# Moving the rotation DMAs to GpSimd and widening the step distances of a hand-ordered two-layer decoder kernel

## The chip, the cores and the metric

The kernel runs on one core of one Trainium2 chip. The metric is the device time of one execution in microseconds (us), as the median of several executions. A profiled execution has a span, from the first instruction to the last one of the core, and a time of its own that is a little longer than the span.

## What is computed

Two layers of a decoder step for one prompt of 512 tokens and eight sample sequences of 4 tokens, which share all weights; the 544 token columns are handled together, in two halves of 272. Everything is float32. A layer is, in short:

```python
h = rmsnorm(x, norm1_g) * (1 + mod[:, 1]) + mod[:, 0]
z = h @ w_in
yA = pool_mixer(z[..., COL_POOL:COL_RET], ...)        # sliding means
q, kr = rotary(zr[:, :, 0], pos), rotary(zr[:, :, 1], pos) * (RET_DK ** -0.5)
yB = retention(q, kr, zr[:, :, 2], st_ret)            # normed, times silu gate
conv_y, n_sc = causal_dwconv(zc[..., 2 * MIX_W:] * zc[..., :MIX_W], st_sc, sc_w)
yC = zc[..., MIX_W:2 * MIX_W] * conv_y
yD = rwkv7_mixer(z[..., COL_RWKV:COL_GATE], ...)      # delta-rule scan over tokens
mixed = jnp.sum(gates * einsum(branches, w_br), axis=2) @ w_out
x = x + mod[:, 2] * mixed
h2 = rmsnorm(x, norm2_g) * (1 + mod[:, 4]) + mod[:, 3]
up = causal_dwconv(h2 @ w_up, st_ffn, ffn_w)
x = x + mod[:, 5] * ((silu(up[..., :D_FF]) * up[..., D_FF:]) @ w_down)
```

`mod` comes from a product of the conditioning with `w_ada`, which the kernel works out beside the rest. The new states of all mixers are outputs too.

## The kernel before

**Large products.** Activations lie with channels on the partitions. A weight arrives in units of 128x1024 (eight tiles of 128x128); its raw copy (three buffers) is split on chip into a high part (a cast on ScalarE, L130) and a low part (a subtraction, L134, on VectorE, for weights 1 and 2 of the start on GpSimd), with four buffer pairs for split weights. Each tile product is three matmuls, high by high, high by low and low by high (L164, L165, L166, `mm3`), on one half of 272 columns. There are 13,248 of these large matmuls. A unit of input projection is 24 large matmuls for each half. Their sums go into three PSUM buffers (`pd`); the small products of the mixers use five others (`pm`).

**The order is written by hand.** Every engine but the DMA-issuing SyncE runs its instructions in the order in which the program emits them. The program counts large matmuls (`nmm`, three at each `mm3`), and after each `mm3` it emits what has come due (`slot`): closures put off by `later(n, ...)` by n large matmuls, and steps of generators, which end in `yield n`. A step thus stands n large matmuls behind the one before, rounded up to the next multiple of three. `yield n, True` marks a step that starts with small matmuls; with a negative n the step is emitted ahead of the others that are due. A distance gives the other engines time to finish what TensorE reads next. `finish` runs what is left of a generator at once.

**The stages of a layer.** First come the eight RWKV input units. Then the generator `rwkv` runs beside the other units: decays and products (`products`, ending in L558, which the small matmuls of L579 read), a substitution of 31 steps on VectorE, and a scan of 16 chunks. A scan chunk goes around TensorE and VectorE: L734 makes `psG`, L696 copies it, L701 multiplies, L705 copies it back, L754 makes the new state, L767 on VectorE adds the decayed old state into `z`, which the next L734 reads; L770 on GpSimd prepares the decayed state `pt` for the chunk after. Beside it come the short convolution, the pooling, their gates (`gates`), and the eight retention units. Of these the first two of each half of the heads, q and k, are rotated: the unit lands in `qn` (L1329), four DMAs (L1338) copy it into `qs` with blocks of 32 partitions swapped, L1339 (VectorE) multiplies `qn` by a cosine table, L1340 (GpSimd) `qs` by a sine table, and L1341 (VectorE) adds both. The tables come by a GpSimd DMA (L1323) for each such unit. After the last chunk GpSimd issues the output of the state (L793) and clears two tiles (L796), which L800 reads; then `retentions` runs. The rest is the output projection, the second norm, and the feed-forward part: up units, whose results go through `conv3` (L1148, L1151, L1152), a silu (L1407), a product (L1411, L1413) and a split (L456, L457), and down products in four parts. A down group is 24, 12, 12 or 18 large matmuls in the four parts, and each ends in a residual on VectorE (L408, L412, L415), which frees its PSUM buffer.

**Norms.** `both_halves` runs eight groups for each half and sums squares (L322, L325); the norm of the first half (`norm_half`: reciprocal L355, multiply L361, scale L338, split L366 and L369) is emitted step by step beside the second half's groups.

**The start.** The first modulation, its eight parts of 1 MB, and the first norm run tile by tile with the first three weight units (`first_units`); weight 3 (the fourth) is loaded when the first three units are done.

Of the kernel before, what the change touches and what calls it, by code (L numbers as in the profile page):

```python
# [24 lines left out]
NU = 138  # L25
D_G, D_S, D_P = 14, 14, 18
KAPPA = -math.exp(-0.5)
# [16 lines left out]
def tile_hybrid_step(ctx: ExitStack, tc: tile.TileContext, io: dict):  # L44
# [305 lines left out]
    def norm_half(xt, half, acc, sA, shA, hh):  # L350

        c0, c1 = HS[half]
        rs = rstd_sqrt(acc)
        yield -8
        V.reciprocal(rs, rs)  # L355
        yield -10
        us = {}
        for i in range(11):
            if i < 8:
                us[i] = ZR(HALF)  # L360
                V.tensor_tensor(out=us[i], in0=xk(xt, i)[:, c0:c1], in1=rs, op=MUL)  # L361
            if 0 <= i - 1 < 8:
                mod_samples(us[i - 1], i - 1, half, sA, shA)
                mod_prompt(us[i - 1], i - 1, half, sA, shA)
            if 0 <= i - 2 < 8:
                S.copy(hilo_of(i - 2, half, hh)[0], us[i - 2])  # L366
            if 0 <= i - 3:
                hi, lo = hilo_of(i - 3, half, hh)
                V.tensor_tensor(out=lo, in0=us[i - 3], in1=hi, op=SUB)  # L369
            yield -11 if half == 0 else -7  # L370

# [87 lines left out]
    def rwkv(l, za, zb, M, yD):  # L459
# [104 lines left out]
        bkn = products(0, e1)  # L564
        yield 44, True
        for T in range(5):
# [35 lines left out]
            if T < 4:  # L602
                yield -14
                bkn = products(T + 1, e1)
                yield 40, True
        rks = []
# [52 lines left out]
        for s in range(31):  # L659
            substitute(s)  # L660
            if s % 2:
                yield -20, False, s > 28
        for h in range(2):
# [142 lines left out]
        for p in range(2):  # L806
# [6 lines left out]
            Zxs.append(Zx)  # L813
        yield 44, True
        psY = PM()
# [46 lines left out]
    def retention(l, p, rt, M, yB):  # L862
# [19 lines left out]
        for ps in pss:  # L882
# [3 lines left out]
            sms.append(sm)  # L886
        yield 24, True
        ps = PM()
# [19 lines left out]
        for T in range(1, 4):  # L908
# [6 lines left out]
                        in1=cst[0:64, C_BM:C_BM + 8].unsqueeze(2).broadcast_to([64, NB, 64]), op=MUL)  # L915
        yield 24, True
        psO = PM()
# [31 lines left out]
        G.dma_start(io["o_ret_s"][l, :, p], S0)  # L949
        yield 24  # L950
        rs = ZR(TOK)
# [74 lines left out]
    for k in range(8):  # L1026
        if k + 4 < 8:
            raw_first(k + 4)
        if k:
            next(afs[k])  # L1030
        if k >= 2:
            first_units(k - 2)
        next(afs[k])
        for half in (1, 0):
            mod_samples(xh0[k][half], k, half, scl[0][:, 0], mods[0][:, 0:8, :])
            mod_prompt(xh0[k][half], k, half, scl[0][:, 0], mods[0][:, 0:8, :])
        if k < 7:
            normed(k + 1)
        for half in range(2):
            hi, lo = hilo_of(k, half, hh)  # L1040
            S.copy(hi, xh0[k][half])
            V.tensor_tensor(out=lo, in0=xh0[k][half], in1=hi, op=SUB)
        if k < 2:
            for _ in range(1 + k):
                load_next(0)
# [7 lines left out]
    for l in range(L):  # L1053
# [91 lines left out]

        def conv3(u, wcol):
            cv = ZR(560)
            S.activation(cv, u[:, 0:560], AF.Copy, scale=wcol(0))  # L1148

            def rest():  # L1150
                V.scalar_tensor_tensor(out=cv, in0=u[:, 1:561], scalar=wcol(1), in1=cv, op0=MUL, op1=ADD)  # L1151
                V.scalar_tensor_tensor(out=cv, in0=u[:, 2:562], scalar=wcol(2), in1=cv, op0=MUL, op1=ADD)  # L1152
            later(5, rest)
            return cv
# [157 lines left out]
        for j, uid in enumerate(RET_UNITS):  # L1312
# [23 lines left out]
            if kind < 2:  # L1336
                for blk in range(4):
                    S.dma_start(qs[32 * blk:32 * blk + 32, :], qn[32 * (blk ^ 1):32 * (blk ^ 1) + 32, :])  # L1338
                V.tensor_tensor(out=qn, in0=qn, in1=tb[0], op=MUL)  # L1339
                later(20, lambda qs=qs, t=tb[1]: G.tensor_tensor(out=qs, in0=qs, in1=t, op=MUL))  # L1340
                later(36, lambda o=rt[:, kind, :], qn=qn, qs=qs: V.tensor_tensor(out=o, in0=qn, in1=qs, op=ADD))  # L1341
            done(l, ui - 1)
# [56 lines left out]
        def finish_up(j):  # L1399
            cvs = []  # L1400
            for s in range(2):
                wc = P_FFW + 3 * (22 * s + j)
                cvs.append(conv3(upads.pop((j, s)), lambda t, wc=wc: par[:, wc + t:wc + t + 1]))
            if j % 2 == 0:
                acts[j // 2] = T4(F32R)
            a = acts[j // 2]
            later(22, lambda: S.activation(cvs[0], cvs[0], AF.Silu))  # L1407

            def product():
                pr = ZR(TOK)  # L1410
                V.tensor_tensor(out=pr[:, 0:SEQ], in0=cvs[0][:, 0:SEQ], in1=cvs[1][:, 0:SEQ], op=MUL)  # L1411
                sv = [cv[:, 512:560].rearrange("p (b t) -> p b t", t=6)[:, :, 2:6] for cv in cvs]
                V.tensor_tensor(out=smp(pr[:, SEQ:TOK]), in0=sv[0], in1=sv[1], op=MUL)  # L1413
                later(8, lambda: split_hilo(pr, a[:, 2 * (j % 2), :], a[:, 2 * (j % 2) + 1, :]))
            later(30, product)

# [284 lines left out]
```

## Time and profile before

| what | value |
|---|---|
| median of 3 runs | 2018.62 us (2017.16 to 2023.3) |
| profiled execution, its own time | 2021.17 us |
| its span | 2019.4 us |
| mean granted TensorE clock | 0.983 |
| VectorE busy | 1098.5 us (54%) |
| ScalarE busy | 807.6 us (40%) |
| GpSimd busy | 236.8 us (12%) |
| HBM read | 213.33 MB, 110 GB/s over the span |

TensorE is PE in the profile, its weight loads PEld, VectorE DVE, ScalarE ACT, GpSimd POOL, SyncE SP; a q behind a name is that engine's queue when it issues DMAs. Idle time of an engine is put down to what ended it, the releaser. PEclk is the share of full clock that TensorE was granted in a stretch.

### The profile page before, as it was taken

The page shows a single profiled execution, that of the slowest core. Times are in us where ns is not written, and L with a number is a line of the kernel's source. Part 1 is how long each engine was busy: PE and PEld are TensorE (multiplying, and loading weights), DVE is VectorE, ACT ScalarE, POOL GpSimd, SP SyncE. Part 2 cuts the span into 40 slices and gives each one's busy share as a digit, 9 for nine tenths or more (in the row PEclk, how much of TensorE's full clock was granted, in tenths as well). Part 3 has the DMA queues.
Part 4 walks back from the last instruction along what each step waited for, and adds up shares of the span by engine and source line. Part 5 has one row for each costly group of instructions (what it writes and reads, how often), then busy time and mean ns, then how long its engine had stood idle before and what let it go on. Part 6 is the DMA issues. An engine that isn't in the chain of part 4 may idle for free. (4 is left out here: it accounts for less than half of the span.)

```text
span 2019.4 us, 39097 instructions
## 1 busy us (share of the span) xinstructions
PE 1927.6 (95%) x16188; PEld 1847.3 (91%) x16188; DVE 1098.5 (54%) x2245; ACT 807.6 (40%) x1578; POOL 236.8 (12%) x655
## 2 busy tenths in 40 slices
PE   6999998999999999999989999999899999999997
PEld 5989997879999998899989899988899999999997
DVE  4455754443466553455664667554435755445565
ACT  4543232253355431434345433333524554243432
POOL 1100033212000000000101001442110000000000
PEclk9999999999999999999999999999999999999998
DMA  7223434422334258522332133232124222222221
GB/s 304 86 74 116 129 117 147 139 81 89 128 112 147 78 206 320 200 84 85 106 118 85 54 95 89 65 119 88 59 94 144 86 74 86 100 85 76 94 93 45
DMA packets 75554, 227.15 MB, mean 112 GB/s; under 512 B 20208, under 2 KB 23072, under 8 KB 73584
## 3 DMA queue, kind: packets, MB, share of 16 engines
q1 hardware_dynamic: 69872, 210.43, 31.0%
q0 software_dynamic: 3536, 11.53, 1.7%
q10 hardware_dynamic: 1968, 2.69, 0.5%
q8 instruction: 127, 2.08, 0.4%
q14 instruction: 51, 0.42, 0.1%
HBM read 213.33 MB, written 9.06 MB: 110 GB/s over the span
## 5 line engine op out<-in xcount | busy, mean ns | idle before, releaser
L164 PE MATMUL pd<-t,whi 128*128 128x272 f32 x4104 | 1212.5, 295 | 20.8 <-DVE t L408 9.3
L166 PE MATMUL pd<-t,wlo 128*128 128x272 f32 x4104 | 1194.6, 291 | 4.6 <-POOL wlo L134 2.4
L165 PE MATMUL pd<-t,whi 128*128 128x272 f32 x4104 | 1188.7, 290 | 4.4 <-DVE t L369 3.9
L164 PEld LDWEIGHTS pd<-t,whi 128*128 128x128 f32 x4104 | 780.4, 190 | 55.1 <-issue 22.6
L165 PEld LDWEIGHTS pd<-t,whi 128*128 128x128 f32 x4104 | 782.2, 191 | 7.0 <-DVE t L369 4.8
L166 PEld LDWEIGHTS pd<-t,wlo 128*128 128x128 f32 x4104 | 780.7, 190 | 5.8 <-POOL wlo L134 3.1
L134 DVE TENSOR_TENSOR wlo<-raw,whi 128x1024 fp32r<-128x1024 f32 x256 | 321.6, 1257 | 125.6 <-ACT whi L130 123.4
L130 ACT CAST whi<-raw 128x1024 fp32r<-128x1024 f32 x258 | 270.7, 1051 | 169.5 <-PE pd L165 142.1
L1151 DVE SCALAR_TENSOR_TENSOR zr<-zr,par,zr 128x560 f32<-128x560 f32 x92 | 73.5, 799 | 165.2 <-ACT zr L1148 165.2
L1247 ACT ACTIVATE zr<-pd 128x272 f32<-128x272 f32 x128 | 50.7, 397 | 225.1 <-PE pd L166 213.9
L1395 ACT COPY zr<-pd 128x272 f32<-128x272 f32 (+2 forms) x264 | 72.5, 310 | 155.6 <-PE pd L166 155.6
L408 DVE SCALAR_TENSOR_TENSOR t<-pd,mod,t 128x272 f32<-128x272 f32 (+1 forms) x160 | 76.4, 481 | 92.3 <-PE pd L166 92.2
L1397 POOL COPY off<-zr 128x18 f32<-128x18 f32 x88 | 25.8, 293 | 646.7 <-ACT zr L1395 646.7
L1227 DVE TENSOR_TENSOR zr<-pd,zr 128x272 f32<-128x272 f32 x96 | 40.7, 436 | 84.3 <-PE pd L166 83.8
L1152 DVE SCALAR_TENSOR_TENSOR zr<-zr,par,zr 128x560 f32<-128x560 f32 x92 | 73.8, 802 | 3.3
L456 ACT CAST t<-zr 128x544 fp32r<-128x544 f32 x48 | 31.1, 648 | 108.2 <-DVE zr L1413 108.1
L322 ACT ACTIVATE zr<-t 128x272 f32<-128x272 f32 (+1 forms) x72 | 32.4, 455 | 97.6 <-DVE t L408 55.6
L1229 POOL TENSOR_TENSOR t<-t,zr 128x272 f32<-128x272 f32 x64 | 57.9, 920 | 112.1 <-DVE zr L1227 106.5
L1148 ACT ACTIVATE zr<-zr,par 128x560 f32<-128x560 f32 x92 | 65.8, 767 | 8.8 <-DVE zr L1177 8.8
L164 PE MATMUL pd<-t,t 128*128 128x272 f32 x224 | 64.8, 289 | 1.7 <-DVE zs L412 1.7
L166 PE MATMUL pd<-t,t 128*128 128x272 f32 x224 | 64.6, 288 | 0.0
L165 PE MATMUL pd<-t,t 128*128 128x272 f32 x224 | 64.4, 288 | 0.0
(284 smaller groups left out, 1756.8 us busy)
## 6 DMA issues: line engine op xcount, KB each, us to landing
raw<-in_wst SPq DMA_DIRECT2D x276, 512.0 KB, 3.4
t<-in_wada SPq DMA_DIRECT2D x32, 1024.0 KB, 9.3
raw<-in_wada SPq DMA_DIRECT2D x24, 512.0 KB, 3.6
zr<-in_rope POOLq DMA_DIRECT2D x16, 272.0 KB, 5.0
t<-in_wada SPq DMA_DIRECT2D x8, 512.0 KB, 6.8
t<-in_xT SPq DMA_DIRECT2D x4, 544.0 KB, 6.2
zr<-zr ACTq DMA_DIRECT2D x32, 68.0 KB, 2.1
t<-in_xT SPq DMA_DIRECT2D x2, 1088.0 KB, 8.7
```

What stands on the lines that cost most here:

```text
L130: S.copy(hi, raw)
L134: (G if (l, u) in ((0, 1), (0, 2)) else V).tensor_tensor(out=lo, in0=raw, in1=hi, op=SUB)
L164: PE.matmul(ps, lhsT=a, rhs=xh, start=first, stop=False)
L165: PE.matmul(ps, lhsT=a, rhs=xl, start=False, stop=False)
L166: PE.matmul(ps, lhsT=b, rhs=xh, start=False, stop=last)
L408: V.scalar_tensor_tensor(out=x[:, c0:c0 + npc], in0=ps[:, :npc], scalar=gate[:, m, 0:1], in1=x[:, c0:c0 + npc], op0=MUL, op1=ADD)
L1148: S.activation(cv, u[:, 0:560], AF.Copy, scale=wcol(0))
L1151: V.scalar_tensor_tensor(out=cv, in0=u[:, 1:561], scalar=wcol(1), in1=cv, op0=MUL, op1=ADD)
L1152: V.scalar_tensor_tensor(out=cv, in0=u[:, 2:562], scalar=wcol(2), in1=cv, op0=MUL, op1=ADD)
L1229: (V if last else G).tensor_tensor(out=a[:, c0:c1], in0=a[:, c0:c1], in1=gs, op=ADD)
L1247: S.activation(gs, ps[:, :HALF], AF.Sigmoid)
L1395: pad_evac(lambda o, i, sl: S.copy(o, i), u, ps, half, 2)
```

## The change

Nothing is added to or taken from the computation. It moves instructions, and it moves 32 DMAs from ScalarE's queue to GpSimd's.

```diff
-D_G, D_S, D_P = 14, 14, 18
+D_G, D_S, D_P = 15, 15, 18
...
-            yield -11 if half == 0 else -7
+            yield -8 if half == 0 else -7
...
         bkn = products(0, e1)
-        yield 44, True
+        yield 54, True
...
                 bkn = products(T + 1, e1)
-                yield 40, True
+                yield 50, True
...
             substitute(s)
             if s % 2:
-                yield -20, False, s > 28
+                yield -18, False, s > 28
...
             Zxs.append(Zx)
-        yield 44, True
+        yield 60, True
...
-        if k < 2:
-            for _ in range(1 + k):
+        if k < 3:
+            for _ in range((2, 1, 1)[k]):
                 load_next(0)
...
-        def conv3(u, wcol):
+        def conv3(u, wcol, n=5):
...
-            later(5, rest)
+            later(n, rest)
...
                 for blk in range(4):
-                    S.dma_start(qs[32 * blk:32 * blk + 32, :], qn[32 * (blk ^ 1):32 * (blk ^ 1) + 32, :])
-                V.tensor_tensor(out=qn, in0=qn, in1=tb[0], op=MUL)
-                later(20, lambda qs=qs, t=tb[1]: G.tensor_tensor(out=qs, in0=qs, in1=t, op=MUL))
-                later(36, lambda o=rt[:, kind, :], qn=qn, qs=qs: V.tensor_tensor(out=o, in0=qn, in1=qs, op=ADD))
+                    G.dma_start(qs[32 * blk:32 * blk + 32, :], qn[32 * (blk ^ 1):32 * (blk ^ 1) + 32, :])
+                later(36, lambda qn=qn, t=tb[0]: V.tensor_tensor(out=qn, in0=qn, in1=t, op=MUL))
+                later(36, lambda qs=qs, t=tb[1]: G.tensor_tensor(out=qs, in0=qs, in1=t, op=MUL))
+                later(52, lambda o=rt[:, kind, :], qn=qn, qs=qs: V.tensor_tensor(out=o, in0=qn, in1=qs, op=ADD))
...
-                cvs.append(conv3(upads.pop((j, s)), lambda t, wc=wc: par[:, wc + t:wc + t + 1]))
+                cvs.append(conv3(upads.pop((j, s)), lambda t, wc=wc: par[:, wc + t:wc + t + 1], 16 + 14 * s))
...
-            later(22, lambda: S.activation(cvs[0], cvs[0], AF.Silu))
+            later(34, lambda: S.activation(cvs[0], cvs[0], AF.Silu))
...
-            later(30, product)
+            later(46, product)
```

In `retention`, which runs four times, the three distances `yield 24, True`, `yield 24, True` and `yield 24` become 36. `yield -11` to `-8` is the pace of the first half's norm. Because the count moves in threes, 14 and 15 both come due at 15: the scan's chunks stand exactly where they stood, 48 large matmuls apart. The other distances become, in large matmuls: products to their small matmuls 45 to 54 and 42 to 51, substitution 21 to 18, retention 24 to 36, norm 12 to 9, convolution 6 to 18 and 30, silu 24 to 36, product 30 to 48, end of the scan 45 to 60.

**VectorE at the first rotated unit of a layer.** `qn` is zr_3743 in both orders; z are the scan's states, vt the values that go into them, wlo a weight's low part. Before:

```order
L688 COPY z_3835<-vt_3724 32x64 x4
L1339 TENSOR_TENSOR zr_3743<-zr_3743,zr_3745 128x544
L767 TENSOR_TENSOR z_3605<-pm_3881,pt_3768 64x128
L767 TENSOR_TENSOR z_3606<-pm_3881,pt_3768 64x128
L134 TENSOR_TENSOR wlo_3863<-raw_3860,whi_3862 128x1024
L696 COPY gs_3926<-pm_3923 32x64 x2
L1341 TENSOR_TENSOR t_498_3742<-zr_3743,zr_3744 128x544
L705 COPY z_3606<-pm_3947 32x64 x2
L1339 TENSOR_TENSOR zr_3865<-zr_3865,zr_3867 128x544
```

And after:

```order
L688 COPY z_3835<-vt_3724 32x64 x4
L767 TENSOR_TENSOR z_3605<-pm_3880,pt_3768 64x128
L767 TENSOR_TENSOR z_3606<-pm_3880,pt_3768 64x128
L134 TENSOR_TENSOR wlo_3862<-raw_3859,whi_3861 128x1024
L696 COPY gs_3924<-pm_3921 32x64 x2
L1339 TENSOR_TENSOR zr_3743<-zr_3743,zr_3745 128x544
L705 COPY z_3606<-pm_3946 32x64 x2
L1341 TENSOR_TENSOR t_498_3742<-zr_3743,zr_3744 128x544
L767 TENSOR_TENSOR z_3834<-pm_3979,pt_3889 64x128
```

L1339, which overwrites what the rotation DMAs read, stood ahead of the scan's L767 and now stands behind L767, a weight's subtraction and the copy L696.

**GpSimd at the last rotated unit of a layer.** zr_4188 and zr_4300 (zr_4299 after) are the `qs` of the last two rotated units, pn the scan's last state. Before:

```order
L1323 DMA zr_4302<-in_rope 128x544
L770 TENSOR_TENSOR pt_4324<-z_4054,dec_596 64x128
L770 TENSOR_TENSOR pt_4324<-z_4055,dec_596 64x128
L1340 TENSOR_TENSOR zr_4188<-zr_4188,zr_4190 128x544
L1340 TENSOR_TENSOR zr_4300<-zr_4300,zr_4302 128x544
L793 DMA o_wkv_p<-pn_4458 128x128
L796 MEMSET z_4272 64x128
L796 MEMSET z_4273 64x128
```

And after:

```order
L1323 DMA zr_4301<-in_rope 128x544
L770 TENSOR_TENSOR pt_4323<-z_4053,dec_602 64x128
L770 TENSOR_TENSOR pt_4323<-z_4054,dec_602 64x128
L1340 TENSOR_TENSOR zr_4188<-zr_4188,zr_4190 128x544
L1338 DMA zr_4299<-zr_4298 32x544 x4
L793 DMA o_wkv_p<-pn_4457 128x128
L796 MEMSET z_4272 64x128
L796 MEMSET z_4273 64x128
L1340 TENSOR_TENSOR zr_4299<-zr_4299,zr_4301 128x544
```

The four issues L1338 are new ahead of L793 and L796, and the last L1340 has moved behind them.

**ScalarE in the start**, from the third modulation part on: whi_242 is weight 2's high part, whi_302 that of weight 3; pm_247 and pm_302 (pm_307 after) are sums of the modulation. Before:

```order
L130 CAST whi_242<-raw_118 128x1024
L255 COPY t_16_120<-pm_247 128x256
L338 ACTIVATE t_8_102<-t_8_102,mod_97,scl_99 128x240
L338 ACTIVATE t_8_102<-t_8_102,mod_97,scl_99 128x272
L1041 CAST t_31_174<-t_8_102 128x272 x2
L255 COPY t_16_120<-pm_302 128x256
```

And after:

```order
L130 CAST whi_242<-raw_118 128x1024
L255 COPY t_16_120<-pm_247 128x256
L338 ACTIVATE t_8_102<-t_8_102,mod_97,scl_99 128x240
L338 ACTIVATE t_8_102<-t_8_102,mod_97,scl_99 128x272
L1041 CAST t_31_174<-t_8_102 128x272 x2
L130 CAST whi_302<-raw_300 128x1024
L255 COPY t_16_120<-pm_307 128x256
```

Weight 3's cast, which stood behind the twelve copies that empty the first three units' sums, now stands among the modulation's steps. Its load, on SyncE, is issued ahead of the last modulation part, and waits there until a raw buffer is free.

More of the change, by code (lines that the diff above doesn't have):

```diff
@@ L886, in retention @@
             sms.append(sm)
-        yield 24, True
+        yield 36, True
         ps = PM()
@@ L915, in retention @@
                         in1=cst[0:64, C_BM:C_BM + 8].unsqueeze(2).broadcast_to([64, NB, 64]), op=MUL)
-        yield 24, True
+        yield 36, True
         psO = PM()
@@ L949, in retention @@
         G.dma_start(io["o_ret_s"][l, :, p], S0)
-        yield 24
+        yield 36
         rs = ZR(TOK)
```

## Prediction

> **What bounds the kernel now.** I read the busy shares, then what TensorE waited for, then windows around each wait with the granted clock, then the timeline inside.
>
> ```profile
> PE 1927.6 (95%) x16188; PEld 1847.3 (91%) x16188; DVE 1098.5 (54%) x2245; ACT 807.6 (40%) x1578; POOL 236.8 (12%) x655
> 1650.00:1700.00 50.00, 50.00 (x400) 50.00 (x400) 29.09 (x38) 24.54 (x50) 3.87 (x24) 1.00 0.27 86
> ```
>
> TensorE is busy 95% of the span, and in a full stretch it starts 400 large matmuls in 50 us, 125 ns each. The work itself is not changed, so only TensorE's idle time and its slow clock can be won: 2019.4 - 1927.6 = 92 us idle, and the clock's mean of 0.983. What ended the idle time:
>
> ```profile
> PE pd L164 <- DVE t L408: 9.3, 4, 2.4
> PE pm L734 <- DVE z L767: 9.2, 4, 2.9
> PE pm L445 <- ACT zr L946: 6.1, 2, 3.1
> PE pm L579 <- DVE zr L558: 4.1, 2, 2.0
> PE pd L164 <- ACT whi L130: 3.2, 1, 3.2
> PE pm L896 <- ACT t L874: 3.1, 2, 1.6
> ```
>
> These (total us, times, longest) are short gaps at few places, most of them once per layer. Windows around them (length, then PE's busy time, and the granted clock in the third column from the right):
>
> ```profile
> 55.00:80.00 25.00, 20.92 (x142) 20.27 (x141) 10.32 (x14) 14.33 (x30) 2.04 (x13) 0.86 0.33 106
> 118.00:146.00 28.00, 24.87 (x278) 22.93 (x277) 19.67 (x40) 7.93 (x16) 2.32 (x9) 0.88 0.26 79
> 330.00:372.00 42.00, 36.44 (x326) 33.30 (x326) 17.93 (x52) 11.39 (x32) 14.75 (x29) 0.96 0.54 177
> 372.00:410.00 38.00, 33.48 (x321) 29.66 (x320) 16.77 (x35) 9.44 (x24) 8.77 (x11) 0.91 0.38 120
> 425.00:470.00 45.00, 39.76 (x373) 36.03 (x370) 19.57 (x34) 26.72 (x41) 6.64 (x10) 0.96 0.21 66
> 850.00:880.00 30.00, 28.00 (x226) 26.50 (x219) 18.00 (x39) 8.05 (x12) 0.38 (x3) 1.00 0.22 71
> 975.00:1002.00 27.00, 24.57 (x184) 24.36 (x183) 16.47 (x34) 8.31 (x15) 7.20 (x15) 0.94 0.42 139
> 1035.00:1070.00 35.00, 29.69 (x199) 27.80 (x198) 27.48 (x77) 21.90 (x50) 0.59 (x6) 0.90 0.43 155
> 1124.00:1150.00 26.00, 22.88 (x265) 22.21 (x264) 19.91 (x41) 7.83 (x16) 2.33 (x9) 0.93 0.18 62
> 1330.00:1362.00 32.00, 28.33 (x248) 26.86 (x247) 16.47 (x46) 9.34 (x25) 11.11 (x18) 0.95 0.36 111
> 1362.00:1400.00 38.00, 35.13 (x316) 32.55 (x316) 17.29 (x37) 9.86 (x26) 10.67 (x17) 0.91 0.30 93
> 1415.00:1460.00 45.00, 39.66 (x368) 35.93 (x366) 19.55 (x34) 26.69 (x41) 6.63 (x10) 0.96 0.20 66
> 1815.00:1840.00 25.00, 22.58 (x168) 22.37 (x167) 15.36 (x35) 7.18 (x10) 0.38 (x3) 0.93 0.27 85
> 1940.00:1960.00 20.00, 17.57 (x141) 17.35 (x140) 13.71 (x30) 6.03 (x9) 0.74 (x2) 1.00 0.32 108
> ```
>
> A gap costs more than itself: after most gaps the clock falls for some microseconds. I price a window as its idle time plus length times (1 - clock); this counts the clock twice where TensorE idles at a low clock, so it is a little high. The start: 4.1 + 3.5 = 7.6 us. The first products, two layers: 6.5 + 4.9 = 11.4. The rotations: 7.2 + 7.9 + 5.3 + 6.3 = 26.7. Retention: 7.0 + 7.1 = 14.1. The down groups: 2.0 + 4.1 + 4.2 + 2.4 = 12.7. The layer boundary: 5.3 + 3.5 = 8.8. Together 81 us, the most that the change can win.
>
> **The change part by part.**
>
> Rotations. L1339 overwrites what the rotation DMAs read, so VectorE stands still until they are done, with the scan's L767 behind it:
>
> ```profile
> 330.47 1.13 POOL L1323 DMA_DIRECT2D zr<-in_rope  x2
> 333.52 2.52 ACTq L1338 DMA_DIRECT2D zr<-zr  x4
> 334.13 0.45 PE L754 MATMUL pm<-z,t 64*64 64x64 f32 x8
> 339.48 0.72 DVE L1339 TENSOR_TENSOR zr<-zr,zr 128x544 f32<-128x544 f32 x1 [4.60 <-DMA zr<-zr]
> 340.24 0.61 DVE L767 TENSOR_TENSOR z<-pm,pt 64x128 f32<-64x128 f32 x2
> 340.58 0.81 PE L734 MATMUL pm<-z,t 128*128 128x128 f32 x4 [2.63 <-DVE z L767]
> 340.67 1.74 POOL L770 TENSOR_TENSOR pt<-z,dec 64x128 f32<-64x128 f32 x2 [9.07 <-DVE z L767]
> 390.66 1.88 POOL L1340 TENSOR_TENSOR zr<-zr,zr 128x544 f32<-128x544 f32 x1 [7.23 <-DMA zr<-zr]
> DVE zr L1339 <- DMA zr<-zr: 36.5, 8, 5.9
> ```
>
> L754 is over at 334.6, L767 starts at 340.2. With L1339 emitted behind L767, L767 follows L754 at once, and TensorE's four waits on L767 go. At the layer's last rotation GpSimd itself waits 7.2 us for the DMAs, ahead of L796, for which L800 then waits 4.5; that wait moves behind L796 and goes too.
>
> ```profile
> 393.34 0.80 PE L800 MATMUL pm<-z,t 128*128 128x128 f32 x2 [4.52 <-POOL z L796]
> 383.97 0.39 ACT L1329 COPY zr<-pd 128x272 f32<-128x272 f32 x1 [0.37 <-PE pd L166]
> 392.49 0.57 POOL L793 DMA_DIRECT2D o_wkv_p<-pn  x1
> o_wkv_p<-pn POOLq DMA_DIRECT2D x2, 64.0 KB, 1.8
> ```
>
> What comes late next is GpSimd: it now issues the four DMAs. A pair of its issues takes 1.13 us, so four 2.3: from 333.5 to 335.8, then the two tables of the next unit to 336.9, then L770, 1.7. L770 feeds only the next chunk's L767. At the last rotation the q copy ends at 384.4 by the same clock, issues end at 386.7, L793 and L796 at 387.8; L800 was ready at 393.34 - 4.52 = 388.8. A margin of 1 us. Landing isn't shown for such a DMA from GpSimd. Nearest row: 1.8 us for 64 KB to memory; worst: L1339 came 3.4 us after ScalarE's last issue ended (333.52 + 2.52 = 336.0). So they land between 337.6 and 339.2. VectorE reaches L1339 behind L696 of the next chunk, whose L734 was ready at 340.58 - 2.63 = 337.95 and takes 0.8, so shortly before 339: an estimate of no wait, or up to 0.9 us. I take 24 of the 26.7, and charge 8 x 0.9 = 7 for waits at L1339 and new ones on GpSimd; the bounds of this part are 10 us lost and 27 won. ScalarE loses the issues, with nobody behind that TensorE waited for.
>
> [...]
>
> Start. Weight 3 is cast among the modulation's steps, its load goes out when GpSimd has freed a raw buffer. Before, its cast stood behind the copies: the 3.2 us of L130. The 7.6 go. Beside it, weight 1's cast moves ahead, which lets GpSimd's two subtractions start earlier, and ScalarE has one cast more in the modulation's chain; I set these against each other, and take 7 for the clock counted twice, bounds 4 and 9.
>
> First products. The 9 large matmuls more ahead of L579 are 9 x 0.125 = 1.1 us per layer of the 2.0 wait; the gap before it (VectorE's chain) stays. 2.2, and part of the clock: 4, bounds 2 and 11.
>
> Retention. Twelve matmuls, 1.5 us, more ahead of each step: L445 waits 3.1 to 1.6, L896 1.6 to 0.1, in each layer 3 us, and of the clock most: 9, bounds 6 and 14.
>
> Down groups. At the first groups of 12 large matmuls (1.5 us each) VectorE has the last up unit's work in front of the residual that frees a PSUM buffer:
>
> ```profile
> 858.46 0.80 DVE L1151 SCALAR_TENSOR_TENSOR zr<-zr,par,zr 128x560 f32<-128x560 f32 x1 [7.52 <-ACT zr L1148]
> 862.71 0.50 DVE L408 SCALAR_TENSOR_TENSOR t<-pd,mod,t 128x272 f32<-128x272 f32 x1
> 863.26 0.39 PE L164 MATMUL pd<-t,whi 128*128 128x272 f32 x1 [2.00 <-DVE t L408]
> ```
>
> From 858.46 to 862.71, 4.2 us, it works on the convolution's passes (0.8 each) and a weight, and then frees the first buffer. With the passes due 18 and 30 matmuls later, the first residual goes ahead of them, and each of the next groups finds its buffer freed in time. VectorE's work stays, so some of the wait may come back later: 9 of 12.7, bounds 0 and 12.7.
>
> Layer boundary. The norm's steps come 33 large matmuls sooner by the end, but VectorE is busy 27.5 of these 35 us and the residuals must pass too: 4 of 8.8, bounds 0 and 8.8.
>
> The rest is nothing: the scan's 15 for 14 falls on the same multiple of three; the substitution's faster pace makes good the products' slower one, so the scan starts at the same matmul; 60 for 45 at its end only delays retention, which has the next gates as cover.
>
> Sum: 24 + 7 + 4 + 9 + 9 + 4 - 7 = 50 us. The profiled execution took 2021.17 (span 2019.4), so it would take 1971; the median is 2018.6, 2.5 lower, so **1969**. With no charge and the rest of the clock at three places (5, 3 and 2 us): 67, 1952. The forecast's own range is 1952 to 1984.
>
> The clock is the least sure. Gaps of 2.43 us cost 1.6 in one window (0.94) and nothing in another (1.00). [...]
>
> **The rivals.** (1) *Wider distances only shift the waits*: VectorE has the same work, 20 of 28 us busy at the first products and 27 of 35 at the boundary, and products, retention, down groups and boundary give nothing. For it: their waits are on VectorE or ScalarE. Against: these are busy 54 and 40% over the span, and the work is bunched. 24 + 7 - 7 = 24: 1995. Chance 0.17. (2) *The rotation still blocks*: DMAs from GpSimd land so late that VectorE stands at L1339 as before, one copy later, and L705 comes late in place of L767. For it: up to 5.9 us of wait now. Against: 4.5 us more distance. A third of the rotations' gain: 8 + 33 = 41, 1978. Chance 0.12. (3) *GpSimd becomes the scan's bound*, slower than before: with x for an issue, six issues, L770 (1.7) and L1340 (1.4) must fit into a chunk of 8.4 us (L754 to L754 where nothing waits).
>
> ```profile
> 358.28 0.45 PE L754 MATMUL pm<-z,t 64*64 64x64 f32 x8
> 366.65 0.45 PE L754 MATMUL pm<-z,t 64*64 64x64 f32 x8
> ```
>
> Up to x = 0.88 they fit; the other parts give 33 us, 4.1 for each of eight rotations, of which 1.7 would be clock (as in the windows 330 to 372 and 1330 to 1362), so from 0.88 + 2.4 / 6 = 1.3 us an issue the kernel is slower; at 1.7 us it loses 8 x (4.9 + 1.7) = 53 against 33: 2039. Against: 0.57 in every row. Chance 0.03. (4) Nothing moves, since the gaps are set elsewhere: 0.02. For the forecast 0.66.
>
> **How the numbers follow.** From 1952 to 1996 lie nine tenths of the forecast, all of (2) and half of (1): 0.59 + 0.12 + 0.09 = 0.8. About 0.3%, 6 us, is what a measurement here tells from no change; faster by more have forecast, (1) and (2), 0.95; the same (4), 0.02; slower (3), 0.03.
>
> **What would show it.** In the new profile: no wait of L734 on L767 and of L800 on L796; L1338 in POOLq at about 0.57 us an issue; L1339 behind DMAs for less than 1 us; no wait on L130 near 60 us and clock 1.00 there; L445 at 1.6 us, L579 at 0.9; L408 below 4 in sum. Wrong it is if L705 or L770 turns up among TensorE's releasers, if POOLq's issues take over 0.9 us, or if the clock still falls at the old places.

## The result, and the profile after

| | before | after |
|---|---|---|
| median of 4 runs | 2018.55 us (2017.16 to 2023.3) | 1985.16 us (1979.89 to 1986.78) |
| ratio of the means | | 0.9826, 95% interval 0.9801 to 0.9851 |
| profiled execution, span | 2021.17, 2019.4 us | 1986.48, 1984.7 us |
| mean granted TensorE clock | 0.983 | 0.989 |

The kernel is 33 us faster. The forecast was 50 us, 1969. The result lies inside the wide range, 1952 to 1996, and 1 us outside the forecast's own, 1952 to 1984; it is 7 us from what rival (2) gave (1978) and 10 us from rival (1) (1995). The list of what ended TensorE's idle time in the kernel after (total us, times, longest) shows what is new:

```profile
PE pd L164 <- DVE zr L1227: 20.9, 16, 4.1
...
PE pd L164 <- DVE zs L412: 4.0, 4, 1.7
PE pm L926 <- DVE t L907: 3.6, 2, 1.8
PE pm L579 <- DVE zr L558: 1.8, 2, 0.9
PE pd L165 <- DVE t L369: 1.7, 2, 1.3
```

The waits on L767, L796, L408, L130, L946 (by L445) and L874 are gone, 38 us in all. The wait on L1227, the gates' evacuation of a PSUM buffer, was 4.5 us before and is 20.9 now. The windows of the kernel after that answer to those of before (length, PE's busy time, and the granted clock in the third column from the right):

```profile
40.00:80.00 40.00, 39.91 (x389) 39.05 (x388) 20.99 (x45) 23.84 (x54) 4.01 (x16) 1.00 0.25 85
110.00:140.00 30.00, 28.01 (x322) 26.52 (x322) 25.41 (x55) 9.43 (x18) 3.82 (x14) 1.00 0.34 103
320.00:360.00 40.00, 40.00 (x430) 36.50 (x429) 20.59 (x59) 12.90 (x35) 20.96 (x41) 0.99 0.60 192
360.00:400.00 40.00, 40.00 (x338) 36.10 (x338) 18.47 (x37) 16.73 (x33) 9.02 (x14) 0.97 0.38 126
400.00:470.00 70.00, 59.92 (x528) 56.01 (x527) 28.76 (x49) 31.20 (x52) 11.22 (x15) 0.93 0.21 66
840.00:870.00 30.00, 30.00 (x241) 29.84 (x240) 20.12 (x46) 8.00 (x11) 0.24 (x3) 1.00 0.27 89
1010.00:1050.00 40.00, 33.66 (x246) 32.20 (x245) 30.08 (x83) 25.75 (x57) 0.60 (x6) 0.96 0.38 136
1100.00:1130.00 30.00, 28.01 (x316) 27.34 (x315) 26.02 (x56) 9.32 (x18) 3.79 (x14) 1.00 0.22 72
1310.00:1345.00 35.00, 35.00 (x355) 33.93 (x354) 17.40 (x48) 11.57 (x33) 16.35 (x32) 0.95 0.42 133
1345.00:1380.00 35.00, 35.00 (x299) 31.93 (x298) 19.14 (x35) 17.45 (x30) 8.14 (x13) 1.00 0.25 78
1380.00:1450.00 70.00, 59.89 (x514) 55.17 (x514) 26.87 (x47) 29.77 (x48) 11.24 (x15) 0.90 0.20 66
```

Priced as in the prediction, idle time plus length times (1 - clock), each stage stands as follows; the three other down groups read like the window from 840, TensorE busy throughout at clock 1.00.

| stage | lost before | lost after | won | forecast |
|---|---|---|---|---|
| start | 7.6 | 0.1 | 7.5 | 7 |
| first products | 11.4 | 2.0 + 2.0 = 4.0 | 7.4 | 4 |
| rotations | 26.7 | 0.4 + 1.2 + 1.8 + 0 = 3.4 | 23.3 | 24 - 7 = 17 |
| retention | 14.1 | 15.0 + 17.1 = 32.1 | **-18.0** | 9 |
| down groups | 12.7 | 0 | 12.7 | 9 |
| layer boundary | 8.8 | 6.3 + 1.6 = 7.9 | 0.9 | 4 |
| sum | 81.3 | 47.5 | 33.8 | 50 |

The sum, 33.8, meets the 34.7 between the two profiled executions. One row carries the error: retention lost 18 us where it was to win 9. The timelines of the changed kernel at the first of its new waits, start and length in us, first VectorE:

```profile
419.53 0.73 DVE L954 TENSOR_TENSOR t<-t,zr 128x544 f32<-128x544 f32 x1 [8.08 <-ACT zr L453]
...
422.37 0.43 DVE L1227 TENSOR_TENSOR zr<-pd,zr 128x272 f32<-128x272 f32 x1
```

ScalarE:

```profile
414.28 1.28 ACT L450 ACT_TABLE_LOAD   x1
...
417.55 1.28 ACT L453 ACT_TABLE_LOAD   x1
418.84 0.66 ACT L453 ACTIVATE zr<-zr 128x544 f32<-128x544 f32 x1
...
421.71 1.28 ACT L1247 ACT_TABLE_LOAD   x1
```

And TensorE:

```profile
422.86 0.39 PE L164 MATMUL pd<-t,whi 128*128 128x272 f32 x1 [1.63 <-DVE zr L1227]
...
427.20 0.59 PE L164 MATMUL pd<-t,whi 128*128 128x272 f32 x1 [2.57 <-DVE zr L1227]
...
454.26 0.48 PE L164 MATMUL pd<-t,whi 128*128 128x272 f32 x1 [4.11 <-DVE zr L1227]
```

The last step of a retention emits TensorE's small products L445, ScalarE's ln and exp (L450, L453) and VectorE's L954 in one go. So VectorE stands 8 us at L954 until L453 is done, and L1227, which frees the PSUM buffer that TensorE wants, stands behind it in VectorE's order. Some 4.5 of the 8 us lie ahead of the step's L445 and cost nothing; from the start of L445 to the end of L1227 it is 6.9 us at this place and 8.1 us at the next. The first stall comes in two waits, 1.6 and 2.6 us, the second in one of 4.1. The trace of before had such a stand too, but TensorE then wanted nothing that stood behind it:

```profile
438.21 0.73 DVE L954 TENSOR_TENSOR t<-t,zr 128x544 f32<-128x544 f32 x1 [5.22 <-ACT zr L453]
```

Counted in TensorE's order, the last steps stood behind large matmul 2196 and 2286 of the first layer, now behind 2250 and 2376. The gates beside them are units of 24, whose sums ScalarE's L1247 evacuates, and short ones of 6, which VectorE's L1227 evacuates. By the same count four short units end at 2262, 2268, 2274 and 2280; from there on the period is 60, two units of 24 and then a short pair, which ends at 2334 and 2340, 2394 and 2400, 2454 and 2460. So 2250 lies 6 matmuls ahead of the first short unit, and 2376 lies 12 ahead of a pair; TensorE waits behind 2268, 2280 and 2400. In the order of before, 2196 and 2286 lay 60 and 42 ahead.

The stalls are 16.6 of the 20.2 us that TensorE idles in the two retention windows. The other 3.6 are the waits of L926 on VectorE's L907; they shrink to 1.6 with the scan's end 84 behind, and are not there with 120, or with the old distances of 24. What causes them stays open.

### The profile page after: what moved, and what is told of

The parts are those of the page before. It is cut to its first block, busy times and chain, and to the rows that moved or that the text cites. A ratio compares the mean times of both kernels' runs of the same rounds, so it can differ in the third digit from the quotient of the medians.

```text
span 1984.7 us, 39086 instructions
## 1 busy us (share of the span) xinstructions
PE 1914.8 (96%) x16188; PEld 1837.4 (93%) x16188; DVE 1097.5 (55%) x2245; ACT 813.6 (41%) x1578; POOL 244.9 (12%) x687
## 4 chain that ended last, share of the span: by engine, by line
PE 88%; DVE 7%; ACT 3%; issue 1%; DMA 0%; POOL 0%; DVEq 0%; SPq 0%; ACTq 0%
PE pd L164 27%; PE pd L166 26%; PE pd L165 26%; PE pm L282 2%; DVE wlo L134 1%; PE pm L734 1%; DVE zr L325 1%; PE pm L754 1%; DVE zr L1227 1%; ACT L453 1%; PE pm L758 1%; PE pm L579 0%; PE pm L586 0%; ACT zr L322 0%; ACT zr L450 0%
## 5 line engine op out<-in xcount | busy, mean ns | idle before, releaser
L164 PE MATMUL pd<-t,whi 128*128 128x272 f32 x4104 | 1210.5, 295 | 23.7 <-DVE zr L1227 20.9
L134 DVE TENSOR_TENSOR wlo<-raw,whi 128x1024 fp32r<-128x1024 f32 x256 | 320.7, 1253 | 299.6 <-ACT whi L130 297.2
L130 ACT CAST whi<-raw 128x1024 fp32r<-128x1024 f32 x258 | 270.6, 1051 | 146.6 <-PE pd L165 139.2
L1247 ACT ACTIVATE zr<-pd 128x272 f32<-128x272 f32 x128 | 50.6, 397 | 215.8 <-PE pd L166 215.4
L408 DVE SCALAR_TENSOR_TENSOR t<-pd,mod,t 128x272 f32<-128x272 f32 (+1 forms) x160 | 76.7, 480 | 85.8 <-PE pd L166 85.4
L1397 POOL COPY off<-zr 128x18 f32<-128x18 f32 x88 | 19.9, 226 | 645.6 <-ACT zr L1395 645.6
L1227 DVE TENSOR_TENSOR zr<-pd,zr 128x272 f32<-128x272 f32 x96 | 40.7, 436 | 79.1 <-PE pd L166 78.6
L696 DVE COPY gs<-pm 32x64 f32<-32x64 f32 x68 | 15.2, 224 | 64.7 <-ACT gs L696 64.1
```

Of the source, the lines that this page charges most:

```text
L130: S.copy(hi, raw)
L134: (G if (l, u) in ((0, 1), (0, 2)) else V).tensor_tensor(out=lo, in0=raw, in1=hi, op=SUB)
L164: PE.matmul(ps, lhsT=a, rhs=xh, start=first, stop=False)
L408: V.scalar_tensor_tensor(out=x[:, c0:c0 + npc], in0=ps[:, :npc], scalar=gate[:, m, 0:1], in1=x[:, c0:c0 + npc], op0=MUL, op1=ADD)
L1227: V.tensor_tensor(out=a[:, c0:c1] if first else gs, in0=pp[:, :HALF], in1=gs, op=MUL)
```

## The experiments

**Retention: distance or place.** The theory: it is the place of the last step in the gates' period that costs, not the distance. The rivals stand in the expectations. These place the gates' short units at 2256 to 2268, 2316 to 2328 and 2376 to 2388; the later pairs lie 12 matmuls behind that, as counted above. The kernel before, run again beside three groups of these kernels, took 2016.43, 2017.84 and 2018.95 us, so times of different groups compare to within some 2 us; each ratio is to the kernel before of its own group. First, only the whole retention part undone:

```diff
-        yield 60, True
+        yield 44, True
...
-        yield 36, True
+        yield 24, True
...
-        yield 36, True
+        yield 24, True
...
-        yield 36
+        yield 24
```

> The changed kernel with the whole retention part undone: its three steps 24 behind and the scan's end 44, so that the last steps fall at matmuls 2196 and 2286 as in the kernel before. My theory: the 31.9 us lost in the two windows of retention become the 14 of the kernel before, with L445 waiting 3 us per layer for L946 again and no wait on L1227 above 1 us: 1985 - 18 = 1967. Rival, that retention's loss comes from the rotations' or the convolution's part: 1985.

Measured: 1966.21 us (1965.27 to 1967.06), ratio to before 0.974 (0.9725 to 0.9755). Its waits, and windows of 75 us around the two retentions:

```profile
PE pm L445 <- ACT zr L946: 6.1, 2, 3.1
PE pd L164 <- DVE zr L1227: 4.5, 12, 0.9
```

```profile
395.00:470.00 75.00, 71.27 (x649) 67.14 (x648) 33.72 (x57) 36.65 (x58) 13.31 (x18) 0.98 0.20 69
1370.00:1445.00 75.00, 70.55 (x596) 67.12 (x595) 30.87 (x47) 35.11 (x54) 16.15 (x20) 0.98 0.25 82
```

The retention part of the change cost 19 us. Next, its distances alone undone (the three `yield 36` back to 24, `yield 60` kept):

> The changed kernel, but the three steps of a retention stay 24 large matmuls apart (as before) in place of 36. My theory: what counts is where a retention's last step falls among the projections of the gates, not how far behind it is. VectorE stands 8 us at L954 for ScalarE's exp (about 33 large matmuls), and L1227, which frees the gates' PSUM, stands behind it. In the changed kernel the last steps fall at matmuls 2250 and 2376, right ahead of projections at 2256 to 2268 and 2376 to 2388. With 24 they fall at 2214 and 2304: the first has its stall over at 2247, ahead of the projection, the second runs into the one at 2316 to 2328. So of the 31.9 us lost in the two retention windows of the changed kernel, the first stall goes (5.8 and 5.9) and so does the wait of L926 (3.5 and 5.2), the second stall (5.7 and 5.8) stays: 1985 - 20 = 1965. Rival A, the wider distances cost by themselves (buffers held longer, VectorE too busy): all goes back to the 14 of the kernel before, both stalls gone, 1985 - 18 = 1967, with no wait on L1227 over 1 us. Rival B, the loss comes from something else in the change (the rotations' work moved into retention): 1985. The waits tell theory and A apart: the theory has one wait on L1227 of 2 to 4 us per layer left.

Measured: 1970.17 us (1969.06 to 1972.37), ratio 0.9768 (0.9753 to 0.9784):

```profile
PE pd L164 <- DVE zr L1227: 8.3, 12, 2.1
PE pm L445 <- ACT zr L946: 6.7, 2, 3.3
```

One wait on L1227 per layer is left, 2.1 us, as the theory had it and rival A not; the wait of L445 on L946, which I had overlooked, is back, 6.7 us in both layers, which is enough for the 5 us above the expected 1965. So the 36 did what the forecast said of it. Then the other way, later instead of sooner:

```diff
-        yield 60, True
+        yield 84, True
```

> The changed kernel with the scan's end step 84 large matmuls behind in place of 60, so that all of retention comes 24 later still, with its distances of 36 kept. The last steps fall at matmuls 2274 and 2400, behind the projections at 2256 to 2268 and 2376 to 2388. My theory: both stalls of L1227 go (5.8, 5.7, 5.9 and 5.8 us), the wait of L926 stays: 1985 - 23 = 1962. Rival A, that distances as such cost: no better than the changed kernel or worse, 1985 or more. Rival B, that something else of the change causes it: 1985.

Measured: 1962.12 us (1961.89 to 1962.53), ratio 0.9727 (0.9713 to 0.9742). Its waits and its two windows:

```profile
PE pd L164 <- DVE zr L1227: 4.0, 10, 0.9
PE pd L164 <- ACT zr L1247: 3.8, 2, 1.9
```

```profile
395.00:470.00 75.00, 71.66 (x656) 66.97 (x655) 37.03 (x60) 38.83 (x62) 12.84 (x19) 0.98 0.20 69
1370.00:1445.00 75.00, 71.64 (x655) 67.58 (x655) 36.42 (x58) 35.06 (x57) 15.94 (x21) 1.00 0.22 76
```

At 2274, when one of the four short units is left, and at 2400, right behind a pair, the stalls of L1227 are gone with all distances of 36 kept. This is the fastest kernel of the study: 2.7% below the kernel before, 23 us below the change. One period later than the change (`yield 120, True`):

> The changed kernel with the scan's end step 120 large matmuls behind in place of 60. The last steps of the two retentions then fall at matmuls 2310 and 2436, exactly one period of the gates (60 matmuls: two units of 24, then two short ones of 6 that L1227 evacuates) behind those of the changed kernel, 2250 and 2376. My theory, that the place in the period decides: the stalls come back as in the changed kernel, waits of 4 us at each of the two places in each layer, 23 us with their clock; 1976 to 1985, by whether the wait of L926 (9 us with clock) comes back too. Rival, that later is better (more distance to something): as with 84 or better, 1962 or less.

Measured: 1981.92 us (1979.82 to 1982.38), ratio 0.9815 (0.9801 to 0.983). TensorE's waits at the two places in the first layer, one row of its list of waits, and the windows:

```profile
434.33 0.40 PE L164 MATMUL pd<-t,whi 128*128 128x272 f32 x1 [1.54 <-DVE zr L1227]
459.93 0.59 PE L164 MATMUL pd<-t,whi 128*128 128x272 f32 x1 [4.11 <-DVE zr L1227]
```

```profile
PE pd L165 <- DVE t L457: 5.0, 4, 2.3
```

```profile
395.00:470.00 75.00, 66.07 (x582) 60.50 (x582) 31.40 (x55) 38.55 (x60) 10.35 (x15) 0.91 0.17 60
1385.00:1460.00 75.00, 65.47 (x563) 60.68 (x562) 33.04 (x55) 33.24 (x52) 15.83 (x21) 0.91 0.19 64
```

The loss is back, and the wait at the second place is 4.11 us again: 2436 lies 12 ahead of a pair, as 2376 does, so there the place is repeated as the theory asked for. At the first place it is not: 2310 lies 18 ahead of a pair, not 6 ahead of four short units, and the wait is 1.5 instead of 4.2. What makes up the rest is a new wait at the short unit behind 2256, on VectorE's splits L457 (5.0 us over both layers) and ScalarE's L456 (1.7), which the theory did not foresee. These split what the steps behind the scan's end make, and those steps now come 60 later. So a part of this loss is the price of being late. That later is better is refuted.

Two tries to do it better. In one, VectorE's part of the last step comes 30 large matmuls behind the exp:

```diff
         exp_half(rs)
+        yield 30
         V.tensor_tensor(out=o, in0=o, in1=rs, op=MUL)
```

> The changed kernel, with VectorE's part of a retention's last step (L954, L955 and the split) emitted 30 large matmuls behind the ln and exp that it waits for, in place of right behind them. All distances of the change stay. My theory: VectorE reaches L954 when the exp is done, so nothing stands behind it; the stalls of L1227 go (23 us in both layers), the wait of L926 stays, 1985 - 23 = 1962. Rival A and rival B: 1985, the gates' L1227 waits as before since VectorE or ScalarE is simply too busy there.

Measured: 1971.55 us (1968.86 to 1973.92), ratio 0.9774 (0.9757 to 0.9791), 14 us won where the theory said 23. The second stall went, but that step also moved, to 2406. At the first, still 2250, ScalarE (lines are one higher here, L1228 is L1227 and L1248 is L1247):

```profile
419.11 1.28 ACT L1248 ACT_TABLE_LOAD   x1
```

TensorE's waits:

```profile
420.85 0.39 PE L164 MATMUL pd<-t,whi 128*128 128x272 f32 x1 [1.20 <-ACT zr L1248]
423.40 0.60 PE L164 MATMUL pd<-t,whi 128*128 128x272 f32 x1 [1.54 <-DVE zr L1228]
```

VectorE no longer stands at L954 there, and TensorE waits all the same: for ScalarE, whose gate activation stands behind ln, exp and their table loads, and then for L1228, which stands behind a weight's subtraction L134 on VectorE, and that behind ScalarE's cast L130, for which VectorE waits 3.2 us. So the theory was part of the cause: the split took 4.2 us of idle time down to 2.7 at that place, where two engines are blocked, VectorE in its order and ScalarE in its own. In the other try the second retention starts 12 instead of 18 behind the first, on top of the 84 (last steps 2274 and 2394):

> The changed kernel with the scan's end step 84 behind, as in the run at 1962, and the second retention starting 12 instead of 18 large matmuls behind the first, so that the last steps fall at matmuls 2274 and 2394. With 2400 the gate unit that ends at 2412 followed 12 matmuls behind ScalarE's ln and exp with their table loads, and TensorE waited 1.9 us for L1247 in each layer (once with 1.7 us of clock). My theory: with 18 between them, as at 2274 and 2292, that wait goes, 1962 - 5 = 1957. Rival, that ScalarE is late there for other work (its casts): 1962.

Measured: 1963.97 us (1962.06 to 1964.51), ratio 0.9728 (0.9712 to 0.9743), nothing won. The wait on L1247 is gone and L1227 has taken its place:

```profile
PE pd L164 <- DVE zr L1227: 8.3, 12, 2.1
```

The expectation took 2394 to lie behind a pair; it lies between the two units of one, so L1227 of the second stands behind L954, and TensorE waits 2.1 us behind 2424. By place, over all these kernels: 6 to 24 ahead of a short unit (2250, 2376, 2436, 2310, 2304) a last step costs 1.5 to 4.2 us of waits on L1227, and 42 or more ahead (2196, 2214, 2286) no wait on L1227 or L1247 is over 0.5. No run here has both last steps that far ahead together with the distances of 36, so a better place than that of 84 may be left. All retention runs together, priced from their two windows of 75 us:

| kernel | last steps (first layer) | lost in retention | time, us |
|---|---|---|---|
| whole part undone | 2196, 2286 | 11.2 | 1966.2 |
| distances undone | 2214, 2304 | 18.3 | 1970.2 |
| the change | 2250, 2376 | 32.2 | 1985.2 |
| split, 30 behind | 2250, 2406 | 18.3 | 1971.6 |
| 84 | 2274, 2400 | 8.2 | 1962.1 |
| 84, second sooner | 2274, 2394 | 10.7 | 1964.0 |
| 120 | 2310, 2436 | 32.0 | 1981.9 |

Against the change, loss and time go together within 3.5 us, and neither goes with distance. That the place decides the stalls of L1227 is shown by 84, which keeps every distance of 36, and by 120, where the wait of 4.11 us comes back at the same place of the next period.

**Rotations: issuer or distance.** The DMAs issued by ScalarE again (`S.dma_start` for `G.dma_start`), the new distances kept:

> The changed kernel, but the rotation DMAs issued by ScalarE again, as before; the wider distances of the rotation's steps stay. My theory: the distance alone takes away the wait at L1339 (36.5 us of VectorE in the kernel before), the issuer matters little; ScalarE loses 8 x 2.5 = 20 us to issues, but has slack: 1985, at most 1990, and the rotation windows lose under 6 us. Rival, GpSimd as the issuer is what helps, since ScalarE's issues hold up its own work in the scan: most of the 22 us won in the rotations goes again, 2000 to 2007.

Measured: 1986.6 us (1983.47 to 1987.02), ratio 0.9844 (0.9825 to 0.9863). The partner, GpSimd as issuer and the old distances:

```diff
-                later(36, lambda qn=qn, t=tb[0]: V.tensor_tensor(out=qn, in0=qn, in1=t, op=MUL))
-                later(36, lambda qs=qs, t=tb[1]: G.tensor_tensor(out=qs, in0=qs, in1=t, op=MUL))
-                later(52, lambda o=rt[:, kind, :], qn=qn, qs=qs: V.tensor_tensor(out=o, in0=qn, in1=qs, op=ADD))
+                V.tensor_tensor(out=qn, in0=qn, in1=tb[0], op=MUL)
+                later(20, lambda qs=qs, t=tb[1]: G.tensor_tensor(out=qs, in0=qs, in1=t, op=MUL))
+                later(36, lambda o=rt[:, kind, :], qn=qn, qs=qs: V.tensor_tensor(out=o, in0=qn, in1=qs, op=ADD))
```

> The changed kernel with GpSimd still issuing the rotation DMAs, but the three steps of a rotation at their old distances (L1339 at once, 20 and 36). The partner of the run with ScalarE as issuer. My theory, that the distance did it: VectorE stands at L1339 for the DMAs again, 30 us or more in all, with L767 behind it; the rotation windows lose 20 us and more, 1985 + 20 = 2005, or more as GpSimd's own tables stand in front of the issues. Rival, that the issuer did it: 1985.

Measured: 2008.15 us (2001.48 to 2009.66), ratio 0.9941 (0.9921 to 0.9961). What VectorE waited for at L1339, first with ScalarE as issuer, then with the old distances:

```profile
DVE zr L1339 <- DMA zr<-zr: 0.3, 1, 0.3
```

```profile
DVE zr L1339 <- DMA zr<-zr: 30.2, 8, 5.6
```

The distance is worth 23 us; the issuer, at the new distances, is worth 1.4, less than the runs tell apart. At the old distances no run changes the issuer alone.

**Down groups.** The convolution, silu and product at their old 5, 22 and 30:

> The changed kernel with the convolution's passes, its silu and the product at their old distances (5, 22, 30). My theory: the waits of the down groups' first buffers on L408 come back, 9.3 us, 12.7 with the clock: 1985 + 12.7 = 1998. Rival, that the earlier layer norm or another part took these waits away: 1985.

Measured: 1996.98 us (1994.79 to 2002.08), ratio 0.9895 (0.9876 to 0.9914), 11.8 us slower than the change:

```profile
PE pd L164 <- DVE t L408: 9.3, 4, 2.4
```

The four waits are back to the tenth of a microsecond; no other part of the change touched them.

**First products, the fourth weight, the norm's pace.** The first products, decays and substitution back (44, 40, 20):

> The changed kernel with the first products and decays at their old distances (44 and 40) and the substitution's pace at its old value (20 at a time). My theory: the wait at L579 is 2.0 us again, and the clock falls behind it: 6.6 us, 1992. Rival 1, that the idle time alone counts and the clock's fall came from somewhere else: 2.2 us, 1987. Rival 2: nothing, 1985.

Measured: 1987.24 us (1986.61 to 1992.1), ratio 0.985 (0.9832 to 0.9868). The windows at the products:

```profile
110.00:140.00 30.00, 26.89 (x302) 24.95 (x302) 22.61 (x50) 9.36 (x18) 3.69 (x13) 0.94 0.25 90
1105.00:1135.00 30.00, 26.88 (x296) 26.16 (x295) 24.14 (x53) 8.04 (x17) 3.67 (x13) 0.94 0.16 54
```

There 4.9 + 4.9 us are lost where the change loses 4.0, clock falls included: 5.8 us at the place, 2 in the median, 5 by the ratios, whose intervals overlap. The fourth weight as before:

```diff
-        if k < 3:
-            for _ in range((2, 1, 1)[k]):
+        if k < 2:
+            for _ in range(1 + k):
```

> The changed kernel with the fourth weight's load and cast where they were. My theory: the gap at 60 us (L164 waits 3.2 us for the cast of L130) and the clock's fall behind it come back, 7 us: 1992. Rival, that only the idle time is worth something: 3.5 us, 1988. Rival, that the start is set by other work: 1985.

Measured: 1986.17 us (1984.71 to 1989.54), ratio 0.9842 (0.9824 to 0.9859). Its wait, and its windows at the start and at retention:

```profile
PE pd L164 <- ACT whi L130: 3.2, 1, 3.2
```

```profile
40.00:80.00 40.00, 36.24 (x354) 34.62 (x353) 19.25 (x47) 21.49 (x47) 1.62 (x10) 0.90 0.21 70
405.00:480.00 75.00, 64.93 (x588) 60.48 (x587) 30.53 (x52) 36.86 (x59) 11.22 (x16) 0.93 0.18 61
1380.00:1455.00 75.00, 64.89 (x605) 60.48 (x604) 32.30 (x54) 37.34 (x59) 12.01 (x16) 0.98 0.18 62
```

The start loses 3.8 + 4.0 = 7.8 us again, yet the median rose by 1. In this execution the same waits in retention cost 26.9 us instead of 32.2, since the clock fell less behind them (0.93 and 0.98 over the two windows, against 0.93 and 0.91). The idle part, 3.7 us, is shown at the place; whether the clock's part is worth as much in the time is open, for both of these runs, which neither medians nor ratios can tell from the change. Last, the norm's pace (`yield -11`):

> The changed kernel with the first half's norm at its old pace of 11 at a time. In the forecast this pace was worth 4 us at the layer boundary; the boundary's window lost 8.3 us before and 7.8 us after. My theory: the pace only changes which of VectorE's results is late there; at most 1 us, 1985 to 1986. Rival, that it was worth 4 us and something else in the change took them away: 1989.

Measured: 1987.45 us (1981.38 to 1987.99), ratio 0.9839 (0.982 to 0.9858):

```profile
1005.00:1045.00 40.00, 35.14 (x248) 33.34 (x247) 29.88 (x83) 25.33 (x57) 0.59 (x6) 0.91 0.36 136
```

Idle 4.9 and clock 3.6, 8.5 us at the boundary against 7.9: the pace moves waits between L369 and L412 and is worth nothing that shows.

## Why the prediction was right, and where it was not

**Retention, the step that failed.** "Twelve matmuls, 1.5 us, more ahead of each step: L445 waits 3.1 to 1.6, L896 1.6 to 0.1." Both waits went, even entirely, and L445's came back with 24. What the step left out is that a moved step takes its instructions past others: L954 and ScalarE's ln and exp moved with it, and I never asked which evacuation would then stand behind them. The prediction even named "the next gates as cover" for the later retention; the gates are cover for TensorE, but VectorE and ScalarE must serve them. The rows that would have told it were in the trace of before: 5.2 us of stand at L954, and the order shows where the gates' short units fall. The price was 32.1 lost against 14.1. At a better place (84) the same distances lose 8.2, against 14.1 before and 11.2 with the whole part undone: the part could have won 3 to 6 us by the windows, and 4 by the times (1962.1 against 1966.2), not 9.

**Rotations.** Mechanism right, shown by the pair of runs, and the charge of 7 us was not needed: VectorE no longer waits at L1339, which puts rival (2) out, and TensorE shows no wait from the scan's L767 or L796; the 3.4 us that stay are falls of the clock in windows without idle time. The DMAs landed 2.0 us after their issue as a median, within the 1.8 to 3.4 that the estimate used. No run shows the 1.7 us an issue from which rival (3) works out its time; L1338 took 0.51 us an issue against an estimate of 0.57, and that rival is out by this row:

```profile
L1338 POOL DMA_DIRECT2D zr<-zr x32 | 16.2, 512 | 30.7 <-ACT zr L1329 30.6 <-issue 0.2
```

**Down groups.** Right; the allowance for waits that come back later (9 of 12.7) was too careful, none came. **Start.** 7.5 for 7 by the windows, with the clock's part unproven in the time. **First products.** The idle time went as worked out, 2.0 to 0.9; of the clock I had counted a part, and all of it went, 7.4 for 4 by the windows (in the time the run with the old distances bears out 2 to 6). No run shows the 5 us more of clock that the fast end of the range counts; here 3.4 more than the 4 came. **Layer boundary.** Mis-sized: 4 was half of what was there, taken without a reason beyond that; 0.9 came, since VectorE is busy 30 of the 40 us and the wait passes from one of its results to the next.

**The rivals.** Rival (1), that wider distances only shift waits, gave 1995 and was wrong for products and down groups, right for the boundary, and in retention the truth was worse than it: shifted onto something that waited more. One sign that the prediction gave for being wrong came: the clock still falls at two of the old places, retention (0.93 and 0.90) and the boundary (0.96). The total of 1985 lies between it and the forecast by the sum of one loss that no case held and of gains above the estimates: against the forecast -27.0 in retention and -3.1 at the boundary, +6.3 at the rotations, +3.7 at the down groups, +3.4 at the products, +0.5 at the start make -16.2, and 50 - 16.2 = 33.8 is what the windows show. So it is in part luck that the total is near: with the other stages as forecast, the 27 us of retention alone would have made 1996, the edge of the wide range.

## What to carry to other kernels

When a step is emitted later, list everything that it puts into each engine's order, and for each in-order engine ask what will now be queued behind its longest wait; a wait that harms nobody at one place cost 4 us here, and mostly 1.7 us by a fall of the clock, when a PSUM evacuation stands behind it. Look at where the evacuations of the work beside it fall before choosing a distance, and count that in the trace: here later and sooner were both better, and later still was nearly as bad. Taking the consumer's work out of one blocked engine's order helps only in part (4.2 us of idle time to 2.7) while the producer engine (ln, exp and their table loads) stands in front of other evacuations.

## What the runs showed of the hardware

**The clock fell in steps of one size, and not behind each gap.** The granted clock (third column from the right) in two windows of 1 us behind the 4.1 us wait of the changed kernel:

```profile
455.00:456.00 1.00, 1.00 (x6) 1.00 (x6) 0.22 (x1) 1.00 (x2) 0.06 (x1) 0.50 0.00 0
456.00:457.00 1.00, 1.00 (x6) 1.00 (x6) 1.00 (x2) 0.69 (x1) 0.00 (x0) 0.50 0.00 0
```

A fall here is half the clock for about 3.4 us, summed over such windows 1.6 to 1.7 us lost. The two stalls of L1227 in each layer, 4.1 to 4.2 us of idle time (once 3.2), stand in seven kernels of this study, 28 times in all. Of the 19 read in windows of 1 us from the stall to the end of the fall, 16 cost 1.6 to 1.7 us of clock, one 2.6 (in a fall twice as long), two nothing. By an estimate from these numbers this alone can make some us of scatter between executions, of the size of the two effects that stayed open above. Falls also came behind less idle time (2.0 us, some 3 us behind a wait of 1.1, at the products at their old distances, in both layers), and the two stalls that had none, of 4.2 us, are each made of two waits of 1.6 and 2.6 us. At the rotations of the changed kernel the clock fell once in each layer though TensorE was busy throughout (40.00 of 40 us at 0.97, 35.00 of 35 at 0.95). So the length of a single gap does not tell in these runs whether a fall comes. The gaps left at the first products, 2.0 us in sum in each window, stand at clock 1.00.

**ln and exp came behind a table load each.** In ScalarE's timeline above L450 and L453 are each preceded by a load of 1.28 us, and the gate's L1247 by a third, 3.8 us for one retention step; so it is at all four last steps of the changed kernel.

**GpSimd's issues beside VectorE's copies.** In the changed kernel GpSimd issues four DMAs from 322.45 to 324.49 us, beside VectorE's float32 copies L688, which end at 323.57:

```profile
322.45 2.04 POOL L1338 DMA_DIRECT2D zr<-zr  x4 [3.25 <-ACT zr L1329]
```

```profile
321.98 1.59 DVE L688 COPY z<-vt 32x64 f32<-32x64 f32 x8
```

The issue took 0.51 us each there as on average (0.50 to 0.54 over all 32), so beside copies of this size (0.2 us each) no issue shows a hold-up; of long copies no run here says anything.
